# One projection moved behind the inverses' doublings in the order, and one expansion tied on VectorE

## The chip, the cores and the metric

One core of one Trainium2 chip runs the whole program. The metric is the device time of one execution in microseconds; lower is better. Engines are named as in the profile: PE (TensorE), DVE (VectorE), ACT (ScalarE), POOL (GpSimd) and SP (SyncE, here only a DMA queue).

## The reference

One layer of a hybrid decoder in float32, over 1024 prompt tokens and 64 sample tokens (8 sequences of 8):

```
h = x + 1/2 SwiGLU1(rmsnorm(x));  n = rmsnorm(h);  proj = n @ w_in
qkv, z, a, b, q_s, k_s, v_s = split(proj)
o_g = gated delta rule(silu(causal_conv(qkv)), a, b)   # 4 heads of 128, chunked, triangular solve
o_s = sliding-window attention(rope(q_s), rope(k_s), v_s)  # 8 query heads of 64, 2 kv heads, window 128
h += concat(rmsnorm(o_g) * silu(z), o_s) @ w_out
h += 1/2 SwiGLU2(rmsnorm(h));  h += sigmoid(rmsnorm(h) @ ple_gate) * (p @ ple_proj);  y = rmsnorm(h)
```

In the delta rule each chunk of 128 tokens needs the inverse of a lower triangular 128 x 128 matrix per head; then a state S is carried from chunk to chunk. The outputs are y, the states, the convolution's last rows and the attention's caches.

## The kernel before, in words

All 1088 tokens lie along the free axis, in four parts of 272 columns. A projection of w_in by one block of 128 output columns is a tile T, 0 to 21. It takes 4 parts of 24 products (8 blocks of the inner dimension, times three products of high and low halves): 96 matmuls of 128x128 on 128x272, in `proj` (L762), each part in one PSUM buffer of pool pps (two buffers, tag m). DVE then multiplies the part by the norm's factor into SBUF (`plain`, L781, or the convolution's `ev_pre`, L823). Tiles 0 to 11 feed the convolution, 12 to 15 are z, 16 to 19 the attention's queries (xq), 20 its keys (xk), 21 its values. A query or key tile then goes through `rope`: two multiplications and an addition of 128x1088 and four small DMAs.

The weights of a tile arrive by one DMA on SP's queue and are split into halves on ACT and POOL. Two split weights are held at a time; `next_weight` (L1455) after each tile asks for the one two places further on.

The inverses: `solve` (L961) inverts the 32x32 blocks on the diagonals for all chunks on DVE and writes them to DRAM (scrX). `levels` (L998), for a pair of chunks each ("lv", i, b: chunks 2i and 2i+1, in the SBUF tiles from b on), loads the blocks (`load_x`, L991), spreads them over a 128x128 block diagonal (`expand`, L985, on DVE: Em from the first set, Dm from the second) and doubles the block size twice, 32 to 64 to 128. One doubling of a chunk is a group of products plv<-lv,AT (a step's first), a mask on DVE, a second group of products, a subtraction on DVE, and after the first doubling a transpose (L1040) copied by ACT. Pairs 0, 2 and 3 use the same SBUF tiles (9 to 12), so pair 2 waits for pair 0; pair 1 has tiles 4 to 7 and runs beside pair 0. The PSUM pool of each chunk of each pair is a number in a table (`gps`, L932): plv00, plv01 and plv10 are 0, plv11 is 1, plv20 is 3 and plv21 is 4, which is pps, the pool of the projections.

`chain` (L1087, "go") is a step of the state, chunk by chunk: products pKS, pv and pS, with DVE and ACT between them, and pqS, the query with the state. `prep` ("pre") loads a chunk's operands, `outp` ("out") finishes its output.

The order of all this is written by hand in the list ORDER, walked at L1488. It is the order of the program, and it gives the priorities to a planner, which then orders each engine's queue by costs of its own; queues are fixed when the kernel runs. Dependencies without a semaphore (NOSYNC) bind only the order on one engine. `mm` (L175) uses them: while a projection is being written (fill), its matmuls are placed behind gates, the last product of each group in `chain`, 22 to a gate (OPT q). A projection that is written while there are no gates yet isn't bound; tile 16 was one, tile 18 is the first that is bound.

Of the kernel before, what the change touches and what calls it, by code (L numbers as in the profile page):

```python
# [13 lines left out]
ALU = mybir.AluOpType  # L14
# [25 lines left out]
G_F1, G_MIX, G_F2, G_PLE, G_FIN, G_GDN, G_CONV = 0, 8, 16, 24, 32, 40, 41  # L40
G_DT, G_ALOG, G_SINK, G_SKS = 89, 93, 97, 105
NVEC = 107
ORDER = [('T', 5), ('co', 5), ('T', 6), ('co', 6), ('T', 4), ('co', 4), ('T', 7), ('T', 8), ('co', 7), ('sc',), ('co', 8), ('s1', 0), ('s1', 1), ('s1', 8), ('T', 9), ('s1', 4), ('s1', 5), ('s1', 6), ('T', 1), ('co', 9), ('s1', 7), ('co', 1), ('T', 10), ('s1', 3), ('s1', 2), ('T', 11), ('co', 10), ('so', 8, (8,)), ('so', 0, (6, 12, 2, 11)), ('T', 21), ('T', 0), ('co', 11), ('co', 0), ('lv', 0, 9), ('T', 2), ('T', 3), ('co', 3), ('co', 2), ('T', 20), ('cvo',), ('qs',), ('T', 16), ('pre', 0, 0), ('lv', 2, 9), ('lv', 1, 4), ('go', 0), ('pre', 1, 4), ('out', 0), ('lv', 3, 9), ('pre', 2, 0), ('pre', 3, 9), ('go', 1), ('go', 2), ('out', 2), ('go', 3), ('out', 1), ('out', 3), ('pre', 4, 0), ('go', 4), ('pre', 5, 4), ('out', 4), ('lvs',), ('pre', 8, 9), ('go', 5), ('out', 5), ('pre', 7, 4), ('pre', 6, 0), ('go', 6), ('go', 7), ('T', 18), ('end',), ('T', 17), ('out', 6), ('swa', 1, 0, 14), ('T', 14), ('out', 7), ('sa', 0, 8), ('swa', 2, 0, 6), ('sb', 0, 1), ('swa', 2, 1, 2), ('T', 12), ('sa', 1, 7), ('swa', 1, 2, 8), ('sb', 1, 4), ('swa', 0, 2, 3), ('swa', 1, 1, 5), ('swa', 0, 0, 14), ('T', 19), ('sa', 2, 13), ('sb', 2, 6), ('swa', 0, 1, 15), ('sa', 3, 2), ('sb', 3, 7), ('swa', 3, 2, 3), ('so8',), ('swa', 3, 0, 8), ('swa', 3, 1, 0), ('T', 15), ('T', 13), ('swa', 2, 2, 4), ('ml', 0, 0), ('ml', 1, 0), ('ml', 3, 0), ('swl', 16, 10), ('ml', 3, 1), ('ml', 2, 0), ('ml', 7, 0), ('ml', 4, 0), ('swa', 0, 3, 6), ('ml', 6, 0), ('ml', 5, 0), ('sws', 1, 13), ('ml', 1, 1), ('ml', 2, 1), ('swa', 1, 3, 2), ('swa', 2, 3, 9), ('sws', 0, 5), ('swa', 3, 3, 12), ('ml', 4, 1), ('ml', 5, 1), ('wo', 0, 3), ('wo', 4, 0), ('ml', 0, 1), ('swe',), ('wo', 5, 2), ('wo', 6, 6), ('wo', 3, 4), ('ml', 6, 1), ('wo', 7, 1), ('wo', 1, 5), ('wo', 2, 7), ('ml', 7, 1)]
NOSYNC = mybir.DependencyInfo(mybir.DependencyClass.NoSync, mybir.DependencyReason.DATA)
CHAIN = ("so", "lv", "lvs", "pre", "go", "out", "qs")
OPT = dict(m=2, a=1, c=1, g=2, t=2, pkk0=1, pkk1=2, pdc0=0, pdc1=0, plv00=0, plv01=1, plv10=0, plv11=2, plv20=0, plv21=1, plv30=0,
           plv31=2, pkq=0, pW=0, pKS=1, W=0, hc=0, hs=0, hw=0, q=0, ne=6, wp=0, px=3, po=3, pxo=3, pxl=3, pol=3, pxol=3, pv=2, pS=2, pqS=0, pov=0, pxg=0, pb=0, pvs=0, pSs0=0, pSs4=2, pr0=1, pr1=1, pt0=1, pt1=4,
           zp=1)
# [101 lines left out]
def decoder_layer(ctx: ExitStack, tc: tile.TileContext, mix_off, a, o):  # L150
    nc = tc.nc
    V, S, T, G = nc.vector, nc.scalar, nc.tensor, nc.gpsimd
# [13 lines left out]
    ident = cst.tile([P, P], F32, name="ident")  # L166
# [1 line left out]
    ones = ones_r.bitcast(F32)  # L168
    vecs = cst.tile([P, NVEC], F32, name="vecs")

    gates, filled, fill = [], [0], [False]

    newest = [None]

    def mm(out, lhsT, rhs, start=True, stop=True, pin=False):  # L175
        i = T.matmul(out, lhsT=lhsT, rhs=rhs, start=start, stop=stop)  # L176
        if pin and newest[0] is not None:
            tc.add_manual_dep(i.ins, newest[0], NOSYNC, reason="keeps its place behind the products that come first")
        newest[0] = i.ins.name
        if fill[0] and OPT["q"]:  # L180
            at = filled[0] // OPT["q"]
            if at < len(gates):
                tc.add_manual_dep(i.ins, gates[at], NOSYNC, reason="fills the time up to the next step of the state")
                filled[0] += 1
        return i

    def bc(ap, axis, n):
        return ap.unsqueeze(axis).to_broadcast(list(ap.shape[:axis]) + [n] + list(ap.shape[axis:]))
# [561 lines left out]
    cvs, cvo = cvt_[:, :, :24], cvt_[:, :, 24:]  # L750
# [234 lines left out]
    def expand(c, xc, t):  # L985
        n, m = (P, C("bm")) if c < 8 else (NS, C("bm8")[:NS])
        nb = m.shape[1]
        V.tensor_tensor(out=t.rearrange("p h (b r) -> p h b r", b=nb), in0=bc(xc, 2, nb),
                        in1=bc(bc(m, 1, 4), 3, n // nb), op=ALU.mult)

    def load_x(t, c):  # L991
        n, src, q0, bl = (P, scrX, 4 * c, BL) if c < 8 else (NS, scrXs, 0, DT)
# [2 lines left out]
            nc.sync.dma_start(out=xc[:, w], in_=src[w].rearrange("(q p r) -> p q r", p=n, r=bl)[:, q0 : q0 + 4])  # L995
        return xc

    def levels(cs2, b0):  # L998

        R2 = range(len(cs2))  # L1000
        lv = [B(b0 + j, [2, 4, P], "lv") for j in R2]
        Em, Dm = [t[:, 0] for t in lv], [t[:, 1] for t in lv]
        Pt = B(b0 + 2, [2, 4, P], "Pm")
        At = B(b0 + 3, [2, 4, P], "AT")
        H = P // 2

        def halves(x, b, odd):

            lead = "p h" if len(x.shape) == 3 else "p"
            x = x.rearrange(f"{lead} (a two b) -> {lead} a two b", two=2, b=b)  # L1010
            return x[:, :, :, odd] if len(x.shape) == 5 else x[:, :, odd]

        def bank(name, b):
            t = gps("plv", H, key=f"plv{cs2[0] // 2}{name}")
            return t, t.rearrange("p h (a b) -> p h a b", b=b)

        for j, c in enumerate(cs2):
            xc = load_x(Pt[:, j], c)
            nc.sync.dma_start(out=At[:, j], in_=scr_a(c))
            expand(c, xc[:, 0], Em[j])  # L1020
            expand(c, xc[:, 1], Dm[j])
        Pc = [Pt[:, j, :, :H] for j in R2]
        for b in (32, 64):
            mask = halves(C(f"M{b}"), b, 0)
            for j in R2:
                pP, pv_ = bank(j, b)
                for hh in range(4):
                    mm(pP[:, hh], At[:, j, hh], halves(Dm[j][:, hh], b, 0))
                V.tensor_tensor(out=Pc[j].rearrange("p h (a b) -> p h a b", b=b), in0=pv_, in1=bc(mask, 1, 4), op=ALU.mult)
            if b != 64:  # L1030
                for j in R2:
                    pD, pv_ = bank(j, b)
                    for hh in range(4):
                        mm(pD[:, hh], Em[j][:, hh], Pc[j][:, hh])
                    dst = halves(Dm[j], b, 0)
                    V.tensor_tensor(out=dst, in0=dst, in1=pv_, op=ALU.subtract)
                for j in R2:
                    pE = gps("plv", key=f"plv{cs2[0] // 2}{j}")
                    for hh in range(4):
                        T.transpose(pE[:, hh], Dm[j][:, hh], ident)  # L1040
                    S.copy(halves(Em[j], b, 1), halves(pE, b, 1))
            else:
# [44 lines left out]
    def chain(I):  # L1087

        c, n = I["c"], I["n"]
# [4 lines left out]
        if S0 is not None and not OPT["W"]:  # L1094
            pk = gps("pKS")[:n]
            for hh in range(4):
                last = mm(pk[:, hh], I["k"][:, hh], S0[:, hh])
            gates.append(last.ins.name)
            for hh in range(4):
                V.scalar_tensor_tensor(out=I["v"][:, hh], in0=pk[:, hh], scalar=cs["egcn"][:n, c, hh : hh + 1], in1=I["v"][:, hh],  # L1100
                                       op0=ALU.mult, op1=ALU.add)
        pv = gps("pv")[:n]
        for hh in range(4):
            W = S0 is not None and OPT["W"]
            last = mm(pv[:, hh], I["XT"][:, hh], I["v"][:, hh], stop=not W)
            if W:
                last = mm(pv[:, hh], I["k"][:, hh], S0[:, hh], start=False)
        gates.append(last.ins.name)
        S.copy(I["vw"][:, :2], pv[:, :2])
        V.tensor_copy(I["vw"][:, 2:], pv[:, 2:])  # L1110
        pS = gps("pS")
        for hh in range(4):
            last = mm(pS[:, hh], I["kd"][:, hh], I["vw"][:, hh])
        gates.append(last.ins.name)
        if S0 is None:
            V.tensor_copy(S1, pS)
        else:
# [288 lines left out]
    def pre(i, c):  # L1406
        I[c] = prep(i, c)
# [28 lines left out]
    def conv_state():  # L1436
        nc.scalar.dma_start(out=o["conv"], in_=cvo)

    ops = dict(co=lambda m: conv_out(m, cvt[m]), sc=scalars, qs=q_scalars, s1=stage1, so=solve,
               lv=lambda i, b: levels((2 * i, 2 * i + 1), b), lvs=levels_sample, pre=lambda c, b: pre(b, c), go=go, out=out,  # L1440
               end=end_state, cvo=conv_state, swa=swa, swe=swa_end, swl=swa_load, sws=swa_sample, sa=sam_a, sb=sam_b,
               so8=sam_out, ml=mix_split)
    first_tile = next(x[1] for x in ORDER if x[0] == "T")
# [198 lines left out]
```

## Time and profile before

| | us |
|---|---|
| median of 3 runs | 2319.13 (2317.98 to 2320.62) |
| profiled execution | 2326.01 |
| its span, first to last instruction | 2324.2 |

| engine | busy us of the span |
|---|---|
| PE | 2256.2 |
| DVE | 1411.5 |
| ACT | 869.2 |
| POOL | 530.3 |

The profile is of one execution, and an engine's busy time is an average over stages with different limits. Matmuls overlap and their ends are modelled, so a busy PE may be one at half its clock; the granted clock is read beside it. Times of rows are us from the span's start.

### The profile page before, as it was taken

The numbers are of one execution on the slowest core, as the hardware profiler recorded it, in microseconds if no ns is written. First come the engines' busy times: TensorE is split into PE (matmuls) and PEld (weight loads), VectorE is DVE, ScalarE is ACT, GpSimd is POOL, SyncE is SP. The second block draws the span as 40 slices with busy tenths as digits, with TensorE's granted clock in tenths as the row PEclk, the third lists the DMA queues.
The fourth block names the chain that finished last, engine by engine and source line by source line (L and its number), as shares of the span: only waits on it lengthen the run. The fifth ranks groups of instructions, "written<-read, shape, count | busy, mean of one in ns | idle before, by whom it ended". The sixth has DMA issues, their size and how long they took to land. (4 is left out here: it accounts for less than half of the span.)

```text
span 2324.2 us, 43652 instructions
## 1 busy us (share of the span) xinstructions
PE 2256.2 (97%) x17472; PEld 2206.9 (95%) x17472; DVE 1411.5 (61%) x2719; ACT 869.2 (37%) x1694; POOL 530.3 (23%) x448
## 2 busy tenths in 40 slices
PE   8999999999999999989999999999999999999997
PEld 7999999999999899889987799999999999999997
DVE  8866655965423567955554537865556684443567
ACT  6433333434412364322234524433333344332444
POOL 0133332210000334332321000233333220011324
PEclk9999999999999999979987799999999999999998
DMA  5322222366433246265543365322222248433223
GB/s 189 106 80 84 76 74 75 125 230 221 156 104 102 86 140 173 90 165 161 158 146 95 93 195 186 112 76 76 76 84 73 76 157 275 136 111 107 95 95 129
DMA packets 180090, 289.85 MB, mean 125 GB/s; under 512 B 33359, under 2 KB 89679, under 8 KB 179887
## 3 DMA queue, kind: packets, MB, share of 16 engines
q1 hardware_dynamic: 126976, 224.77, 30.8%
q10 hardware_dynamic: 52911, 62.29, 7.7%
q8 instruction: 137, 2.24, 0.4%
q14 instruction: 66, 0.54, 0.1%
HBM read 219.48 MB, written 66.83 MB: 123 GB/s over the span
## 5 line engine op out<-in xcount | busy, mean ns | idle before, releaser
L176 PE MATMUL pd<-xa,t 128*128 128x272 f32 x4224 | 532.8, 289 | 5.5 <-DVE s L462 4.7
L176 PEld LDWEIGHTS pd<-xa,t 128*128 128x128 f32 x4224 | 531.9, 189 | 6.4 <-DVE s L462 5.2
L176 PE MATMUL pm<-xn,t 128*128 128x272 f32 x2112 | 300.2, 298 | 16.1 <-DVE pre L823 7.0
L206 DVE TENSOR_TENSOR t<-raw,t 128x1024 fp32r<-128x1024 f32 x126 | 160.2, 1272 | 247.4 <-ACT t L205 246.8
L176 PEld LDWEIGHTS pm<-xn,t 128*128 128x128 f32 x2112 | 280.5, 195 | 21.9 <-DVE pre L823 8.4
L205 ACT CAST t<-raw 128x1024 fp32r<-128x1024 f32 x148 | 155.0, 1047 | 313.1 <-PE pd L176 236.8
L176 PE MATMUL pS<-lT,hS 128*128 128x272 f32 x900 | 260.4, 289 | 0.0
L176 PE MATMUL pS<-hT,lS 128*128 128x272 f32 x900 | 260.1, 289 | 0.0
L176 PE MATMUL pS<-hT,hS 128*128 128x272 f32 x900 | 259.1, 288 | 0.0
L176 PE MATMUL pA<-hB,lA 128*128 128x272 f32 x600 | 172.6, 288 | 0.0
L206 DVE TENSOR_TENSOR lA<-raw,hA 128x512 fp32r<-128x512 f32 x171 | 137.0, 804 | 58.4 <-ACT hA L205 52.2
L176 PE MATMUL pA<-hB,hA 128*128 128x272 f32 x600 | 172.5, 288 | 0.0
L176 PE MATMUL pA<-lB,hA 128*128 128x272 f32 x600 | 172.1, 287 | 0.0
L176 PEld LDWEIGHTS pS<-hT,hS 128*128 128x128 f32 x900 | 169.6, 188 | 0.0
L176 PEld LDWEIGHTS pS<-hT,lS 128*128 128x128 f32 x900 | 169.3, 188 | 0.0
L176 PEld LDWEIGHTS pS<-lT,hS 128*128 128x128 f32 x900 | 169.2, 188 | 0.0
L205 ACT CAST hA<-raw 128x512 fp32r<-128x512 f32 x171 | 105.8, 620 | 160.2 <-PE pA L176 121.0
L205 ACT CAST hS<-raw 128x512 fp32r<-128x512 f32 x145 | 89.4, 620 | 176.5 <-PE pS L176 153.8
L258 POOL TENSOR_TENSOR r<-r,sq 128x544 f32<-128x544 f32 x28 | 47.1, 1682 | 426.7 <-ACT sq L257 425.5
L206 DVE TENSOR_TENSOR lS<-raw,hS 128x512 fp32r<-128x512 f32 x145 | 127.9, 882 | 18.0 <-ACT hS L205 5.2
L462 DVE TENSOR_TENSOR u<-u,pS 128x272 f32<-128x272 f32 x225 | 91.2, 432 | 54.4 <-PE pS L176 54.1
L176 PEld LDWEIGHTS pA<-lB,hA 128*128 128x128 f32 x600 | 113.0, 188 | 0.0
(364 smaller groups left out, 4712.1 us busy)
## 6 DMA issues: line engine op xcount, KB each, us to landing
raw<-in_gu SPq DMA_DIRECT2D x114, 512.0 KB
raw<-in_dn SPq DMA_DIRECT2D x88, 512.0 KB
scrU<-act ACTq DMA_DIRECT2D x88, 272.0 KB
a<-scrU SPq DMA_DIRECT2D x88, 272.0 KB
raw<-in_gate SPq DMA_DIRECT2D x24, 512.0 KB
raw<-in_w_in SPq DMA_DIRECT2D x22, 512.0 KB
raw<-in_w_out SPq DMA_DIRECT2D x14, 512.0 KB
h<-in_x SPq DMA_DIRECT2D x2, 2176.0 KB
```

What stands on the lines that cost most here:

```text
L176: i = T.matmul(out, lhsT=lhsT, rhs=rhs, start=start, stop=stop)
L205: S.copy(hi, src)
L206: return eng.tensor_tensor(out=lo, in0=src, in1=hi.bitcast(F32), op=ALU.subtract)
L258: G.tensor_tensor(out=self.acc[c], in0=self.acc[c], in1=sq, op=ALU.add)
L462: i_ = V.tensor_tensor(out=I[c][out], in0=I[c][x], in1=pt_, op=ALU.add)
```

## The change

In ORDER, ("lv", 0, 9) moves from behind tile 0's convolution to behind tile 20, that is past tiles 2, 3 and 20 and the transposes of 3 and 2. ("T", 16) moves from ahead of ("pre", 0, 0) to behind ("lv", 2, 9) and ("lv", 1, 4). Cut to these entries, the list changes so:

```
- ... ('co', 0), ('lv', 0, 9), ('T', 2), ('T', 3), ('co', 3), ('co', 2), ('T', 20), ('cvo',), ('qs',),
-     ('T', 16), ('pre', 0, 0), ('lv', 2, 9), ('lv', 1, 4), ('go', 0), ('pre', 1, 4), ...
+ ... ('co', 0), ('T', 2), ('T', 3), ('co', 3), ('co', 2), ('T', 20), ('lv', 0, 9), ('cvo',), ('qs',),
+     ('pre', 0, 0), ('lv', 2, 9), ('lv', 1, 4), ('T', 16), ('go', 0), ('pre', 1, 4), ...
```

The gates become a list of places, one per matmul. Pairs 1 and 2 of the inverses add 8 places after each of 6 groups (four first products, two transposes), 96 in all, which are tile 16's; the state's groups add 22 each as before, so tile 18 and those after it keep theirs. Both expansions of chunk 0 are ordered on DVE behind the last eviction of the last tile written by `plain`, which is tile 20's.

```
-        if fill[0] and OPT["q"]:
-            at = filled[0] // OPT["q"]
-            if at < len(gates):
-                tc.add_manual_dep(i.ins, gates[at], NOSYNC, reason="fills the time up to the next step of the state")
+        if fill[0]:
+            if filled[0] < len(places):
+                tc.add_manual_dep(i.ins, places[filled[0]], NOSYNC, reason="fills the time up to the next step of the state")
                 filled[0] += 1
         return i
+    def gate(i, n):
+        places.extend([i.ins.name] * n)
...
     def plain(dst):
         def ev(pm, c0, wd, r):
-            V.tensor_tensor(out=dst[:, c0 : c0 + wd], in0=pm, in1=r, op=ALU.mult)
+            i = V.tensor_tensor(out=dst[:, c0 : c0 + wd], in0=pm, in1=r, op=ALU.mult)
+            last_ev[0] = i.ins.name
...
     def expand(c, xc, t):
...
+        if c == 0:
+            tc.add_manual_dep(i.ins, last_ev[0], NOSYNC, reason="behind the evictions that are ready while the blocks are on their way")
...
-    def levels(cs2, b0):
+    def levels(cs2, b0, fillers):
...
                 for hh in range(4):
-                    mm(pP[:, hh], At[:, j, hh], halves(Dm[j][:, hh], b, 0))
+                    last = mm(pP[:, hh], At[:, j, hh], halves(Dm[j][:, hh], b, 0))
+                if fillers:
+                    gate(last, fillers)
...
                     for hh in range(4):
-                        T.transpose(pE[:, hh], Dm[j][:, hh], ident)
+                        last = T.transpose(pE[:, hh], Dm[j][:, hh], ident)
+                    if fillers:
+                        gate(last, fillers)
...
-            gates.append(last.ins.name)
+            gate(last, OPT["q"])
...
-               lv=lambda i, b: levels((2 * i, 2 * i + 1), b), ...
+               lv=lambda i, b: levels((2 * i, 2 * i + 1), b, 8 if i in (1, 2) else 0), ...
```

## Rows read from the trace of the kernel before

**Rows 1.** The page: busy time of each engine, share of the span, instructions.
```profile
PE 2256.2 (97%) x17472; PEld 2206.9 (95%) x17472; DVE 1411.5 (61%) x2719; ACT 869.2 (37%) x1694; POOL 530.3 (23%) x448
```

**Rows 2.** The page: granted clock of PE in 40 slices of 58.1 us, in tenths.
```profile
PEclk9999999999999999979987799999999999999998
```

**Rows 3.** Stretches: length; PE, PEld, DVE, ACT, POOL busy; granted clock; DMA share; GB/s.
```profile
997.30:1001.50 4.20, 4.20 (x35) 4.02 (x33) 0.00 (x0) 2.44 (x9) 2.38 (x1) 1.00 1.00 277
1001.50:1004.75 3.25, 0.04 (x1) 0.00 (x0) 1.70 (x4) 1.56 (x9) 0.00 (x0) 0.82 1.13 338
1004.75:1012.80 8.05, 8.05 (x44) 8.00 (x45) 4.16 (x8) 1.10 (x6) 1.00 (x1) 0.65 0.85 217
1012.80:1028.50 15.70, 15.70 (x144) 15.46 (x142) 8.62 (x20) 4.37 (x17) 7.83 (x4) 1.00 0.38 84
1028.50:1030.20 1.70, 0.09 (x2) 0.06 (x2) 1.70 (x3) 0.00 (x0) 1.70 (x1) 1.00 1.05 266
1030.20:1047.40 17.20, 17.20 (x88) 16.63 (x89) 7.54 (x15) 1.12 (x3) 4.11 (x4) 0.52 0.60 185
1047.40:1055.30 7.90, 7.90 (x75) 7.58 (x73) 4.10 (x10) 1.94 (x8) 2.04 (x2) 0.96 0.80 256
997.30:1055.30 58.00, 53.17 (x382) 51.75 (x380) 27.81 (x56) 12.53 (x51) 19.06 (x12) 0.79 0.67 189
```

**Rows 4.** DVE in order of time: start, duration, instruction, idle before it and releaser.
```profile
995.65 0.43 DVE L783 TENSOR_TENSOR xk<-pm,r 128x272 f32<-128x272 f32 x1
1003.05 1.29 DVE L988 TENSOR_TENSOR lv<-Pm,ctile 128x512 f32<-128x512 f32 x2 [6.97 <-DMA Pm<-scrX]
1004.26 0.43 DVE L783 TENSOR_TENSOR xk<-pm,r 128x272 f32<-128x272 f32 x1
...
1006.86 1.90 DVE L988 TENSOR_TENSOR lv<-Pm,ctile 128x512 f32<-128x512 f32 x3 [1.21 <-DMA Pm<-scrX]
...
1028.46 1.29 DVE L1196 TENSOR_TENSOR xq<-xq,rope 128x1088 f32<-128x1088 f32 x1 [1.33 <-DMA rot<-xq]
...
1051.28 0.42 DVE L1029 TENSOR_TENSOR Pm<-plv,ctile 128x256 f32<-128x256 f32 x1 [0.86 <-PE plv L176]
```

**Rows 5.** PE in order of time, from tile 20's end to level 2.
```profile
999.38 1.03 PE L855 MATMUL ptk<-ident,cv 128*128 128x128 f32 x8
...
1004.75 4.45 PE L176 MATMUL pm<-xn,t 128*128 128x272 f32 x18 [3.21 <-DVE xk L783]
...
1012.80 1.90 PE L176 MATMUL plv<-lv,AT 128*128 128x64 f32 x16
...
1025.46 1.14 PE L176 MATMUL plv<-lv,Pm 64*64 64x64 f32 x16
...
1037.50 1.97 PE L176 MATMUL plv<-lv,AT 128*128 128x64 f32 x8
```

**Rows 6.** SP's queue in order of time: the loads of the inverses' blocks.
```profile
997.39 2.62 SPq L995 DMA_DIRECT2D Pm<-scrX  x3
```

**Rows 7.** PE in order of time, in the state steps.
```profile
1054.47 1.06 PE L176 MATMUL pKS<-St,qk 128*128 128x128 f32 x8
...
1078.41 0.68 PE L176 MATMUL plv<-lv,Pm 64*64 64x64 f32 x8
...
1080.01 1.06 PE L176 MATMUL pqS<-St,qk 128*128 128x128 f32 x8
...
1132.60 4.77 PE L176 MATMUL pm<-xn,t 128*128 128x272 f32 x36
```

**Rows 8.** Stretches behind the state steps, columns as in rows 3.
```profile
1171.40:1229.00 57.60, 54.27 (x331) 46.74 (x330) 30.09 (x88) 22.31 (x65) 11.57 (x7) 0.85 0.40 132
1229.00:1266.20 37.20, 33.31 (x198) 26.46 (x198) 18.13 (x64) 21.03 (x59) 4.54 (x3) 0.91 0.38 116
1266.20:1301.00 34.80, 34.80 (x113) 24.75 (x112) 13.63 (x56) 11.44 (x44) 1.91 (x1) 0.50 0.25 79
```

**Rows 9.** The same stretch, projections' buffers alone: length, PE, PEld, DVE, clock, DMA.
```profile
1229.00:1266.20 37.20, 0.87 (x5) 0.68 (x5) 0.44 (x1) 0.91 0.38 116
```

More of the change, by code (lines that the diff above doesn't have):

```diff
@@ L42 @@
 NVEC = 107
-ORDER = [('T', 5), ('co', 5), ('T', 6), ('co', 6), ('T', 4), ('co', 4), ('T', 7), ('T', 8), ('co', 7), ('sc',), ('co', 8), ('s1', 0), ('s1', 1), ('s1', 8), ('T', 9), ('s1', 4), ('s1', 5), ('s1', 6), ('T', 1), ('co', 9), ('s1', 7), ('co', 1), ('T', 10), ('s1', 3), ('s1', 2), ('T', 11), ('co', 10), ('so', 8, (8,)), ('so', 0, (6, 12, 2, 11)), ('T', 21), ('T', 0), ('co', 11), ('co', 0), ('lv', 0, 9), ('T', 2), ('T', 3), ('co', 3), ('co', 2), ('T', 20), ('cvo',), ('qs',), ('T', 16), ('pre', 0, 0), ('lv', 2, 9), ('lv', 1, 4), ('go', 0), ('pre', 1, 4), ('out', 0), ('lv', 3, 9), ('pre', 2, 0), ('pre', 3, 9), ('go', 1), ('go', 2), ('out', 2), ('go', 3), ('out', 1), ('out', 3), ('pre', 4, 0), ('go', 4), ('pre', 5, 4), ('out', 4), ('lvs',), ('pre', 8, 9), ('go', 5), ('out', 5), ('pre', 7, 4), ('pre', 6, 0), ('go', 6), ('go', 7), ('T', 18), ('end',), ('T', 17), ('out', 6), ('swa', 1, 0, 14), ('T', 14), ('out', 7), ('sa', 0, 8), ('swa', 2, 0, 6), ('sb', 0, 1), ('swa', 2, 1, 2), ('T', 12), ('sa', 1, 7), ('swa', 1, 2, 8), ('sb', 1, 4), ('swa', 0, 2, 3), ('swa', 1, 1, 5), ('swa', 0, 0, 14), ('T', 19), ('sa', 2, 13), ('sb', 2, 6), ('swa', 0, 1, 15), ('sa', 3, 2), ('sb', 3, 7), ('swa', 3, 2, 3), ('so8',), ('swa', 3, 0, 8), ('swa', 3, 1, 0), ('T', 15), ('T', 13), ('swa', 2, 2, 4), ('ml', 0, 0), ('ml', 1, 0), ('ml', 3, 0), ('swl', 16, 10), ('ml', 3, 1), ('ml', 2, 0), ('ml', 7, 0), ('ml', 4, 0), ('swa', 0, 3, 6), ('ml', 6, 0), ('ml', 5, 0), ('sws', 1, 13), ('ml', 1, 1), ('ml', 2, 1), ('swa', 1, 3, 2), ('swa', 2, 3, 9), ('sws', 0, 5), ('swa', 3, 3, 12), ('ml', 4, 1), ('ml', 5, 1), ('wo', 0, 3), ('wo', 4, 0), ('ml', 0, 1), ('swe',), ('wo', 5, 2), ('wo', 6, 6), ('wo', 3, 4), ('ml', 6, 1), ('wo', 7, 1), ('wo', 1, 5), ('wo', 2, 7), ('ml', 7, 1)]
@@ new lines @@
+ORDER = [('T', 5), ('co', 5), ('T', 6), ('co', 6), ('T', 4), ('co', 4), ('T', 7), ('T', 8), ('co', 7), ('sc',), ('co', 8), ('s1', 0), ('s1', 1), ('s1', 8), ('T', 9), ('s1', 4), ('s1', 5), ('s1', 6), ('T', 1), ('co', 9), ('s1', 7), ('co', 1), ('T', 10), ('s1', 3), ('s1', 2), ('T', 11), ('co', 10), ('so', 8, (8,)), ('so', 0, (6, 12, 2, 11)), ('T', 21), ('T', 0), ('co', 11), ('co', 0), ('T', 2), ('T', 3), ('co', 3), ('co', 2), ('T', 20), ('lv', 0, 9), ('cvo',), ('qs',), ('pre', 0, 0), ('lv', 2, 9), ('lv', 1, 4), ('T', 16), ('go', 0), ('pre', 1, 4), ('out', 0), ('lv', 3, 9), ('pre', 2, 0), ('pre', 3, 9), ('go', 1), ('go', 2), ('out', 2), ('go', 3), ('out', 1), ('out', 3), ('pre', 4, 0), ('go', 4), ('pre', 5, 4), ('out', 4), ('lvs',), ('pre', 8, 9), ('go', 5), ('out', 5), ('pre', 7, 4), ('pre', 6, 0), ('go', 6), ('go', 7), ('T', 18), ('end',), ('T', 17), ('out', 6), ('swa', 1, 0, 14), ('T', 14), ('out', 7), ('sa', 0, 8), ('swa', 2, 0, 6), ('sb', 0, 1), ('swa', 2, 1, 2), ('T', 12), ('sa', 1, 7), ('swa', 1, 2, 8), ('sb', 1, 4), ('swa', 0, 2, 3), ('swa', 1, 1, 5), ('swa', 0, 0, 14), ('T', 19), ('sa', 2, 13), ('sb', 2, 6), ('swa', 0, 1, 15), ('sa', 3, 2), ('sb', 3, 7), ('swa', 3, 2, 3), ('so8',), ('swa', 3, 0, 8), ('swa', 3, 1, 0), ('T', 15), ('T', 13), ('swa', 2, 2, 4), ('ml', 0, 0), ('ml', 1, 0), ('ml', 3, 0), ('swl', 16, 10), ('ml', 3, 1), ('ml', 2, 0), ('ml', 7, 0), ('ml', 4, 0), ('swa', 0, 3, 6), ('ml', 6, 0), ('ml', 5, 0), ('sws', 1, 13), ('ml', 1, 1), ('ml', 2, 1), ('swa', 1, 3, 2), ('swa', 2, 3, 9), ('sws', 0, 5), ('swa', 3, 3, 12), ('ml', 4, 1), ('ml', 5, 1), ('wo', 0, 3), ('wo', 4, 0), ('ml', 0, 1), ('swe',), ('wo', 5, 2), ('wo', 6, 6), ('wo', 3, 4), ('ml', 6, 1), ('wo', 7, 1), ('wo', 1, 5), ('wo', 2, 7), ('ml', 7, 1)]
@@ L169, in decoder_layer @@
     vecs = cst.tile([P, NVEC], F32, name="vecs")
-    gates, filled, fill = [], [0], [False]
+    places, filled, fill = [], [0], [False]
+    last_ev = [None]
     newest = [None]
@@ L987, in expand @@
         nb = m.shape[1]
-        V.tensor_tensor(out=t.rearrange("p h (b r) -> p h b r", b=nb), in0=bc(xc, 2, nb),
-                        in1=bc(bc(m, 1, 4), 3, n // nb), op=ALU.mult)
+        i = V.tensor_tensor(out=t.rearrange("p h (b r) -> p h b r", b=nb), in0=bc(xc, 2, nb),
+                            in1=bc(bc(m, 1, 4), 3, n // nb), op=ALU.mult)
+        if c == 0:
+            tc.add_manual_dep(i.ins, last_ev[0], NOSYNC, reason="behind the evictions that are ready while the blocks are on their way")
     def load_x(t, c):
@@ L1107, in chain @@
                 last = mm(pv[:, hh], I["k"][:, hh], S0[:, hh], start=False)
-        gates.append(last.ins.name)
+        gate(last, OPT["q"])
         S.copy(I["vw"][:, :2], pv[:, :2])
@@ L1113, in chain @@
             last = mm(pS[:, hh], I["kd"][:, hh], I["vw"][:, hh])
-        gates.append(last.ins.name)
+        gate(last, OPT["q"])
         if S0 is None:
@@ L1439, in decoder_layer @@
     ops = dict(co=lambda m: conv_out(m, cvt[m]), sc=scalars, qs=q_scalars, s1=stage1, so=solve,
-               lv=lambda i, b: levels((2 * i, 2 * i + 1), b), lvs=levels_sample, pre=lambda c, b: pre(b, c), go=go, out=out,
+               lv=lambda i, b: levels((2 * i, 2 * i + 1), b, 8 if i in (1, 2) else 0), lvs=levels_sample, pre=lambda c, b: pre(b, c), go=go, out=out,
                end=end_state, cvo=conv_state, swa=swa, swe=swa_end, swl=swa_load, sws=swa_sample, sa=sam_a, sb=sam_b,
```

## The prediction

> **What bounds the kernel now.** I read the page first: PE is busy 97% of the span [rows 1], so time can only go where PE waits or runs slowly. The row of granted clocks says where: full nearly everywhere but in the 18th slice (988 to 1046 us), the 21st to 23rd (1162 to 1336) and the last [rows 2], the first two where the inverses, and later the attention, are mixed with projections. I then cut that stretch into windows [rows 3]. From 997.3 (end of tile 20's products) to 1055.3 (the second state step) PE does tile 16, the transposes of tiles 3 and 2, levels 0, 1 and 2 and the first state step. Busy time times clock, added over the seven windows, is 4.2 + 0.0 + 5.2 + 15.7 + 0.1 + 8.9 + 7.6 = 41.8 us of work at 2.4 GHz in 58.0 us: 16.2 us are lost, 4.8 by waiting and 11.4 by the 1.2 GHz level.
>
> The reader should see three losses. From 1001.5 to 1004.75 PE stands; its queue's head is tile 16's second part, which needs a PSUM buffer that tile 20's last eviction frees. That eviction (1004.26) stands on DVE behind two expansions that waited 6.97 us for the inverses' blocks [rows 4]. The low clock follows, until about 1011 (0.65 in the window to 1012.8). From 1028.5 to 1030.2 PE does nothing while DVE runs the rope of tile 16 (1.29 us) ahead of a subtraction [rows 4], and then comes 1030.2 to 1047.4: PE busy all the time at a clock of 0.52, on the small products of levels 1 and 2 and one state step [rows 3].
>
> **The change part by part.** *The tied expansion.* DVE runs tile 20's last eviction when its products end, so the wait of 3.2 us before tile 16's second part goes. But tile 16 is no longer there to profit. The expansions of pair 0 need their blocks: the second set of three is released at 1006.86 [rows 4], four loads behind the ones issued at 997.39 [rows 6]. In program order the loads of level 0 move behind the weight loads of tiles 2, 3 and 20; I cost this at nothing, since what they wait for is the solve and not the queue (if a weight load slips between, some 1.2 us, what DVE waited for the last of these loads). The first expansion waits for the same blocks as before; what is behind it on DVE are the other expansions, which wait for them too.
>
> *The hole.* So PE has, from 997.3 until the first product of level 0, only 18 transposes: 8 took 1.03 us [rows 5], 2.3 us in all. The first product is ready when chunk 0's second expansion ends, 1006.86 + 0.7 (one of the three's 1.90, with its end) plus some 0.2, about 1007.8, instead of 1012.80 [rows 5]: the levels start 5.0 us earlier, but 10.5 us hold 2.3 us of work: **8.2 us lost**. Of tile 16 nothing runs here; before, most of it did, and the rest among level 0's products.
>
> *Tile 16 among the doublings.* 96 products at 4.77/36 [rows 7] are 12.7 us. The first 48 are ordered behind level 2's six marked groups, the rest behind level 1's. The text of the kernel speaks against their running there. All parts of a projection use the two buffers of one PSUM pool, and so does the second chunk of level 2 (plv21 is 4, that pool), five times, all five ahead of tile 16 in program order. Whether buffers go round in program order the trace can show: the product of the query with the state of step 1 needs the state that its neighbour pKS used at 1054.47, and runs at 1080.01, just after level 3's last products at 1078.41 [rows 7], whose second chunk shares its pool and stands ahead of it in the program. Buffers do seem to be handed out in program order. Then tile 16's first part waits until level 2's last but one bank is evicted, which was at 1051.28 [rows 4]: it comes behind the doublings, not among them.
>
> *The levels without filler.* The remaining work is 41.8 - 12.7 - 2.3 = 26.8 us, of which 3.6 (1051.7 to 1055.3) can follow tile 16's start: 23.2 us of small products stand between 1007.8 and it. PE comes to them out of the hole; after the waits that end at 1004.75 and 1030.2 the rows show the 1.2 GHz level each time [rows 3], so I start there. How long? Bounds from rows: 8.05 us at 0.65 (2.8 lost; the products after that wait were tile 16's), 17.2 us at 0.52 (8.3 lost; the same products as here), 34.8 us at 0.50 (17.4 lost; the attention's small products with no projection among them [rows 8, 9]). I take the middle of the last two, 26 us: **13 us lost**, because the products are those of the 17.2 but, unlike then, no projection precedes them.
>
> When the clock is back (about 1034) 10 us of work are left, mostly level 2. It reuses level 0's tiles, and from level 0's last product (1025.46 + 1.14) to level 2's first (1037.50) the loads and expansions took 10.9 us [rows 5]. Level 0 should end near 1026 at the low level, so level 2 starts near 1037, level 1 covers all but 1 to 2 us, and the two chunks of level 2 alone wait for each other's evictions: **4 us** of waits (estimate; 1.5 if only the load gap counts, 8 if the clock returns early and the chain alone sets the pace).
>
> Tile 16's own evictions (four), rope, next weight split and five DMAs on ACT's queue, and on SP's queue the load of the weight two ahead, move from 1005 to 1034 into the state steps. No tile waits for them soon. Their cover is DVE's idle time (it is idle half of 997.3 to 1055.3 [rows 3]); uncovered, one rope ahead of a chain step costs the 1.7 us of that window. I take nothing.
>
> *Sum of the stretch.* 8.2 + 13 + 4 = 25.2 us lost against 16.2: **9 us later** at equal work.
>
> *What comes back.* The state steps order the later projections by 22 as before, so about a projection more is left at 1171 and runs among the attention's products. There PE is not short of loss: 37.2 - 33.31 x 0.91 = 6.9 us in 1229 to 1266.2 and 17.4 to 1301 [rows 8], almost without projections [rows 9]. Lower bound 0; upper about 12, half of the 24.3. I take 2: the tail that moves in reaches only from 1229 to about 1240, and the average clock there is 0.91.
>
> Net **+7 us**. The profiled execution took 2326.01 us (span 2324.2 and 1.8 around it), which would be 2333; it stands 0.3% above the median of the runs, 2319.13, so the forecast is **2326**.
>
> **The rivals.** *The clock returns at once.* This is level 0 to 2 at 2.4 GHz after 8 us (2.8 lost); then the chain sets the pace, and the waits are nearer 7. 8.2 + 2.8 + 7 - 16.2 - 2 is about 0: 2319. For it: from 1047.4 the clock is 0.96 on such products [rows 3]. Against it: 17.2 us without a wait at 0.52. The Trainium skill, "TensorE: Matmul & The Clock Gate", section "Why this matters for your kernels", says that matmuls issued back to back keep the PE warm and that waiting between bursts makes it cold. By that rule the hole is a fault of this change and dense doublings are a cure; the trace agrees on the hole, and on the cure only after 1047. By the rule alone the time is this rival's.
>
> *It does what it says.* If buffers are not handed out in order, 48 products of tile 16 fill level 2's waits (4 us back) and end the slow stretch some 6 us sooner (3 us): +7 - 7 = 0: 2319. Against it: the row at 1080.01.
>
> *Low clock until tile 16.* Then 23.2 us of small products run at 1.2 GHz throughout: 23.2 lost, no waits beside it, 2.8 more until tile 16 has raised the clock: 8.2 + 23.2 + 2.8 - 16.2 - 2 = +16: 2335. For it: the 34.8 us at 0.50.
>
> *The late stage takes it in (the other side).* If the projection that is left over keeps the clock up between 1229 and 1301, where 24.3 us are lost, more than 9 us come back and the sign turns; from 14 on it is measurable. At 18 it is +9 - 18 = -9: 2310. For it: 34.8 us at 0.50 with no projection [rows 8, 9]. Against it: nothing ties the leftover to that place; it runs as soon as it can, just behind 1229.
>
> **How the numbers follow.** A change under 0.2% (4.6 us) is about what a measurement of this kernel can't tell from none. Forecast 0.36, its own range 2322 to 2330, about one in eight of it under the bound; clock at once 0.14; as it says 0.14; low until tile 16 0.14; late stage 0.22. Slower: 0.31 + 0.14 = 0.45, and 0.02 from the two at zero, 0.47. Same: 0.05 + 0.23 = 0.28. Faster: 0.22 and 0.03, 0.25. The range runs from the late stage to the low clock, 2309 to 2335.
>
> **What would show it.** In the changed profile: tile 20's last eviction right after its products; PE nearly idle with transposes from about 997 to 1008; level 0's first product near 1008; a granted clock near 0.5 from there for 20 to 35 us; tile 16's products in one run after level 2's last but one eviction, not in eights between the level's groups; about a projection more of products after the last state step. Wrong I am if tile 16's eights stand among level 2's products, if the clock is full by 1016, or if the stretch from 1229 to 1301 has lost its 0.50.

## The result, and the profile after

| | before | after |
|---|---|---|
| median, 16 runs each | 2315.72 us (2300.43 to 2328.88) | 2329.64 us (2321.66 to 2342.99) |
| ratio | | 1.007, 95% interval 1.005 to 1.0091 |
| span of the profiled execution | 2324.2 us | 2327.3 us |

The change makes the kernel 0.7% slower, 14 us by the medians and 16 by the ratio. The forecast was 2326 us, 7 above before.

The page of the kernel after: PE's row of busy times, and the granted clock in 40 slices, now of 58.2 us.

```profile
PE 2262.1 (97%) x17472; PEld 2215.5 (95%) x17472; DVE 1408.9 (61%) x2719; ACT 870.1 (37%) x1694; POOL 532.3 (23%) x448
...
PEclk9999999999999999968999899999999999999999
```

PE has as many instructions as before and 5.9 us more of busy time [rows 1]. The clock is low in the 18th slice (989.1 to 1047.3 us), lower than before, and in the 19th, where it was full; of the 21st to 23rd, which read 8, 7 and 7, only the 23rd is still below, at 8 [rows 2]. Stretches of the kernel after, with the columns of [rows 3]; tile 20's products end at 1002.40 here, and 1079.46 is the state's second step, the point of equal work. The last two lines are stretches of [rows 8].

```profile
1002.40:1012.65 10.25, 3.23 (x18) 2.40 (x17) 3.59 (x7) 5.50 (x26) 3.35 (x2) 0.67 1.04 280
1012.65:1028.20 15.55, 14.28 (x66) 13.90 (x66) 7.32 (x15) 2.83 (x14) 5.52 (x3) 0.50 0.46 119
1028.20:1064.56 36.36, 36.36 (x187) 34.76 (x186) 12.29 (x28) 1.86 (x5) 1.04 (x1) 0.50 0.46 129
1064.56:1078.80 14.24, 14.24 (x106) 14.24 (x105) 7.32 (x21) 1.61 (x8) 2.04 (x2) 0.90 0.25 60
...
1002.40:1079.46 77.06, 68.77 (x380) 65.96 (x378) 30.96 (x71) 12.44 (x53) 11.94 (x8) 0.60 0.49 133
...
1229.00:1266.20 37.20, 37.20 (x262) 32.32 (x261) 17.25 (x62) 20.17 (x55) 3.27 (x2) 1.00 0.31 95
1266.20:1301.00 34.80, 34.80 (x153) 25.49 (x151) 16.89 (x60) 18.63 (x56) 5.53 (x3) 0.66 0.45 146
```

The same products take 77.1 us instead of 58.0 [rows 3]. Busy time times clock is 2.2 + 7.1 + 18.2 + 12.8 + 0.7 = 41.0 us, so 36.1 are lost: 8.1 in the hole, 7.1 + 18.2 = 25.3 by the 1.2 GHz level while the doublings run without a projection, 1.3 by waits among them, 1.4 until tile 16 has brought the clock back. PE in order of time in the same stretch:

```profile
994.68 7.81 PE L177 MATMUL pm<-xn,t 128*128 128x272 f32 x48 [2.07 <-DVE xk L787]
1002.33 1.03 PE L860 MATMUL ptk<-ident,cv 128*128 128x128 f32 x8
...
1012.65 1.97 PE L177 MATMUL plv<-lv,AT 128*128 128x64 f32 x8 [3.98 <-DVE lv L993]
...
1063.52 1.11 PE L177 MATMUL plv<-lv,Pm 64*64 64x64 f32 x8
1064.56 7.53 PE L177 MATMUL pm<-xn,t 128*128 128x272 f32 x48
1071.94 0.83 PE L177 MATMUL pov<-Y,X 128*128 128x128 f32 x6
1072.52 6.26 PE L177 MATMUL pm<-xn,t 128*128 128x272 f32 x48
...
1079.46 1.11 PE L177 MATMUL pKS<-St,qk 128*128 128x128 f32 x8
```

Tile 16 runs behind level 2's last group as one run of 96 products, but for six others between its halves; not one of its eights stands among the doublings. A group of 8 products of level 0 takes 1.97 us, where 16 took 1.90 before [rows 5]. DVE at the end of tile 20:

```profile
1000.49 0.43 DVE L787 TENSOR_TENSOR xk<-pm,r 128x272 f32<-128x272 f32 x1
1007.49 0.69 DVE L993 TENSOR_TENSOR lv<-Pm,ctile 128x512 f32<-128x512 f32 x1 [6.58 <-DMA Pm<-scrX]
1008.11 0.43 DVE L787 TENSOR_TENSOR xk<-pm,r 128x272 f32<-128x272 f32 x1
1008.46 1.28 DVE L993 TENSOR_TENSOR lv<-Pm,ctile 128x512 f32<-128x512 f32 x2
```

Tile 20's last eviction (1008.11) still stands behind an expansion that waits 6.58 us. Only chunk 0's two expansions are tied; another chunk's, which is not, now comes first (with all expansions tied, below, the eviction runs at 1000.65, ahead of every expansion).

From equal work on, the 19.1 us shrink. The last product of the last state step comes 181.7 us after tile 20's end instead of 173.9: 11.3 us were made up among the state steps. 8.9 of these are put off, since 260 projection products are left then instead of 193 (67 at 4.77/36 [rows 7]). So 16.7 us remain, close to the 14 to 16 that the runs measure.

### The profile page after: what moved, and what is told of

The parts are those of the page before. It is cut to its first block, busy times and chain, and to the rows that moved or that the text cites. A ratio compares the mean times of both kernels' runs of the same rounds, so it can differ in the third digit from the quotient of the medians.

```text
span 2327.3 us, 43647 instructions
## 1 busy us (share of the span) xinstructions
PE 2262.1 (97%) x17472; PEld 2215.5 (95%) x17472; DVE 1408.9 (61%) x2719; ACT 870.1 (37%) x1694; POOL 532.3 (23%) x448
```

## The experiments

All ratios are against the kernel before, run beside them. Each run lists its span and its mean granted clock; "all runs" is the mean, over a kernel's runs, of the clock lost, span x (1 - clock), and of the rest of the span. The last two columns tell where the one profiled execution lost its clock: "levels" is 1000 to 1080 us, "attention" 1180 to 1380, each in windows of 20 us, (1 - granted clock) x 20 added up; "idle" is the time in which PE was not busy there.

| run | ratio (95% interval) | all runs: clock lost, rest | span of the profile | levels: clock, idle | attention: clock, idle |
|---|---|---|---|---|---|
| before | | 50.2, 2264.2 | 2324.2 | 12.0, 4.8 | 30.8, 8.1 |
| before again | | | 2328.8 | 12.0, 5.3 | 36.0, 8.8 |
| after | 1.007 (1.005 to 1.0091) | 70.3, 2261.2 | 2327.3 | 30.6, 8.3 | 17.2, 4.3 |
| tile 16 back | 1.0007 (0.9982 to 1.0031) | 45.2, 2264.1 | 2296.9 | 13.6, 6.5 | 1.8, 4.3 |
| only tile 16 moved | 1.0096 (1.0061 to 1.013) | 67.6, 2262.6 | 2320.5 | 29.0, 6.7 | 15.6, 5.5 |
| tile 16 not tied | 1.0095 (1.0061 to 1.0129) | 66.8, 2262.0 | 2322.1 | 30.8, 6.3 | 15.6, 6.9 |
| level 2 in another pool | 1.0165 (1.0132 to 1.0198) | 77.4, 2268.8 | 2352.0 | 24.0, 11.6 | 44.6, 7.2 |
| tile 16 among levels 0, 1 | 1.0105 (1.0072 to 1.0138) | 68.6, 2269.9 | 2340.6 | 12.2, 11.2 | 44.4, 5.3 |
| hole filled | 1.0054 (1.0025 to 1.0082) | 64.1, 2264.2 | 2315.6 | 20.6, 5.8 | 15.6, 1.7 |
| rope late | 1.0068 (1.0039 to 1.0097) | 66.7, 2265.8 | 2332.3 | 10.2, 5.9 | 36.8, 12.1 |
| tile 18 among levels 2, 1 | 1.0025 (0.9994 to 1.0055) | 53.9, 2265.2 | 2314.0 | 8.4, 7.2 | 20.4, 5.7 |
| all tied | 0.9978 (0.9947 to 1.001) | 46.7, 2263.5 | 2311.8 | | |
| chunk 3 late | 0.9971 (0.994 to 1.0001) | 51.3, 2260.2 | 2304.3 | 15.2, 3.9 | 15.6, 3.4 |
| chunk 3 late, again | 0.997 (0.9939 to 1.0002) | 46.6, 2261.2 | 2315.6 | 15.2, 4.9 | 17.0, 4.5 |

The profiled executions of tile 16 back, only tile 16 moved and tile 16 not tied are the fastest of their kernels' runs, and that of hole filled is the second fastest of twelve: they lose 9 to 11 us less clock than these runs do on average. The levels' column repeats between profiles (12.0 twice for before, 15.2 twice for chunk 3 late); the attention's has to be read with the third column beside it.

### Which part of the change costs: tile 16

**Tile 16 back**, level 0 late and the expansions of chunk 0 tied as in the change.

```
-    ('cvo',), ('qs',), ('pre', 0, 0), ... ('lv', 1, 4), ('T', 16), ('go', 0)
+    ('cvo',), ('qs',), ('T', 16), ('pre', 0, 0), ... ('lv', 1, 4), ('go', 0)
-               lv=lambda i, b: levels(..., b, 8 if i in (1, 2) else 0)
+               lv=lambda i, b: levels(..., b, 0)
```

> Tile 16 goes back to its old place, untied, and the levels give no places; level 0's later place in the list and the tie of chunk 0's expansions stay. Theory A (the loss comes from tile 16 having left the wait for the blocks and level 0): about the kernel before, 4 us less to 2 us more, and no stretch of more than 20 us at half clock between tile 20 and the first state step. Theory B (level 0's later place or the tie costs it): as the changed kernel, about 14 us over the kernel before.

It measured 1.0007: as before. **Only tile 16 moved** is the other half, against the changed kernel:

```
-    ('co', 0), ('T', 2), ... ('T', 20), ('lv', 0, 9), ('cvo',)
+    ('co', 0), ('lv', 0, 9), ('T', 2), ... ('T', 20), ('cvo',)
...
-        if c == 0:
-            tc.add_manual_dep(i.ins, last_ev[0], NOSYNC, ...)
```

> Level 0 goes back to its old place in the list and nothing is tied on DVE; only tile 16 is moved, with its places. Theory A: as the changed kernel, 10 to 18 us over the kernel before, with tile 16 in one run behind level 2. Theory B: within 4 us of the kernel before.

It measured 1.0096 and loses 29.0 us of clock in the levels, as the changed kernel does. So tile 16's new place is the whole loss, and the place of level 0 and the tie are worth nothing that shows here. **Tile 16 not tied** leaves the eights out:

```
-            fill[0] = True
+            fill[0] = bound          # False for tile 16
-               lv=lambda i, b: levels(..., b, 8 if i in (1, 2) else 0)
+               lv=lambda i, b: levels(..., b, 0)
```

> The changed kernel without the eights: tile 16 in its new place in the list but bound to nothing, and the levels give no places. Theory A: the eights bind nothing that the buffers don't bind already, so this is the changed kernel within 4 us, 10 to 18 us over the kernel before. Theory C (the eights hold tile 16 back): tile 16 runs before level 2 ends and most of the 14 us come back.

1.0095, with 30.8 us against 30.6: the eights bind nothing.

### Why the eights don't run, and what they would do

**Level 2 in another pool** changes one number of the table of PSUM pools.

```
-    plv21=4
+    plv21=3
```

> The changed kernel with level 2's second chunk in another PSUM pool (plv21 3 for 4), so that tile 16's buffers no longer come after it. Theory A with the buffers as the cause of the late run: tile 16 stands in eights among level 2's groups, and 5 to 9 us of the 14 come back. If the buffers are not what holds tile 16: one run behind level 2 as in the changed kernel, and 14 us over the kernel before.

PE of this kernel among level 2's groups (its tile 20 ends at 997.1):

```profile
1035.72 2.16 PE L177 MATMUL pm<-xn,t 128*128 128x272 f32 x8
...
1043.08 2.16 PE L177 MATMUL pm<-xn,t 128*128 128x272 f32 x8
...
1046.63 1.59 PE L177 MATMUL plv<-Pm,lv 128*128 128x64 f32 x8
...
1053.04 1.27 PE L177 MATMUL pm<-xn,t 128*128 128x272 f32 x8
...
1064.65 1.05 PE L177 MATMUL pS<-Y 128*128 128x128 f32 x8
```

The eights are there, so it was the order in which a pool's buffers are given out that held them, as forecast. Eight products take 2.16 us at 1043 and 1.27 at 1053: the clock returns near 1047, some 11 us after the first eight. But I had expected a gain, and the kernel is 1% slower than the changed one. In the two profiles the levels lose 6.6 us less of clock and 3.3 more by waiting; the attention loses 27.4 us more of clock and 2.9 more by waiting. Over all runs it is less lopsided: 7.1 us more of clock lost than in the changed kernel, and 7.6 us more of the rest.

**Tile 16 among levels 0 and 1** keeps the pools and puts the tile ahead of level 2 in the program.

```
-    ('lv', 2, 9), ('lv', 1, 4), ('T', 16), ('go', 0)
+    ('lv', 1, 4), ('T', 16), ('lv', 2, 9), ('go', 0)
-               ... 8 if i in (1, 2) else 0)
+               ... 8 if i in (0, 1) else 0)
```

> The change with tile 16 ahead of level 2 in the program and its eights tied among levels 0 and 1. The hole behind tile 20 stays. If the loss is that small products run at the 1.2 GHz level until projection products stand among them, the eights bring the clock back near 1025 instead of 1067 and some 8 to 10 of the 14 us are given back: ratio to before 1.001 to 1.004. If the hole alone makes the loss, the ratio stays at 1.007. If eights among the levels push the state steps back, as the run with another PSUM pool for level 2 suggests, it is 1.010 or more.

PE behind the hole:

```profile
1010.35 1.97 PE L177 MATMUL plv<-lv,AT 128*128 128x64 f32 x8 [4.15 <-DVE lv L993]
1012.07 2.16 PE L177 MATMUL pm<-xn,t 128*128 128x272 f32 x8
...
1021.03 1.00 PE L177 MATMUL plv<-Pm,lv 128*128 128x64 f32 x8
...
1061.35 0.71 PE L177 MATMUL plv<-lv,Pm 64*64 64x64 f32 x8 [1.36 <-DVE Pm L1038]
```

In its own stretch the mechanism works: the clock is back at 1021, 11 us after the hole, the levels lose 12.2 us of clock as before the change, and level 2 and tile 16 are through 62.2 us after tile 20's end (999.86 to 1062.06) instead of 76.4 in the changed kernel. Then the attention takes it all, 44.4 us against 17.2; over all runs, too, this kernel loses as much clock as the changed one (68.6 and 70.3). The rest of its span is 8.7 us longer, of which the profile shows 2.9 as waits in the levels. The measured 1.0105 is the last rival's number, but not by its cause: the last state step ends 178.1 us after tile 20's end, only 4.2 later than before, with 189 projection products left (193 before).

### Is it the pause or the small products?

**Hole filled** adds 72 products that nothing reads.

```
+    def dummy(w):                                   # called behind tile 20
+        pm = proj_ps(0, 4)
+        for ci in range(3):
+            acc3(pm[:, : CH[ci][1]], [blocks(w)[k] + nm.x(ci, k) for k in range(KD)])
```

> The change with 72 more products of 128x272, tile 20's again, written behind tile 20 into a PSUM buffer that nothing reads: 9.5 us of added work in the hole. If the pause is what drops the clock and small products keep the level that they come with, levels 0 to 2 run at the full clock: 23 us of loss become some 7 us of waits, level 0 starts up to 2 us later, and the kernel is about 14 us faster than the changed one in spite of the added work: ratio to before about 1.001. If small products lose the clock by themselves, whatever stands ahead of them, it is low again by 1020 and the ratio is 1.007 to 1.009.

```profile
1007.28 1.63 PE L177 MATMUL pm<-xn,t 128*128 128x272 f32 x11
1008.88 2.00 PE L177 MATMUL plv<-lv,AT 128*128 128x64 f32 x16
1013.24 0.71 PE L177 MATMUL pkq<-qk 128*128 128x128 f32 x4 [2.35 <-DMA qk<-scrT]
...
1017.99 3.68 PE L177 MATMUL plv<-Pm,lv 128*128 128x64 f32 x16 [3.49 <-DVE Pm L1038]
...
1055.80 0.60 PE L1049 MATMUL plv<-ident,lv 128*128 128x128 f32 x4
```

Level 0 begins at the full clock (16 products in 2.00 us) and comes out of two pauses of 2.35 and 3.49 us at half of it (16 in 3.68). So small products did not lose the clock at once, and it fell across two pauses; the hole is one of several pauses, and filling it only puts the fall off to 1018. The full level is back near 1055, after 38 us at half clock without a projection. The trace doesn't part the theories, since "low again by 1020" was the second one's sign. The measured 1.0054, up to 1.0082, leaves out the 1.001 of the first and not the 1.007 of the second, and the profiled execution, at 2317.38, stands 15 us under the median of its twelve runs.

### The attention stage

**Before again** is the kernel before, unchanged.

> The kernel before, unchanged, for a second profile. If the low clock from 1200 to 1320 of its first profile (about 30 us lost) is of that execution and not of the program, this one differs there by more than 5 us, and its span differs by as much; if it is the program's, it shows the same windows again.

Nearly the same windows and a span 4.6 us longer, short of the bound of 5 us: no answer. Both profiled executions of before lie high among its 86 runs beside the experiments (2298.64 to 2340.48, median 2315.73), and the runs tell more. Each lists its mean granted clock, from 0.967 in the longest to 0.987 in the shortest; span x (1 - clock) has a correlation of 0.96 with the time. Averaged, the kernel before loses 50.2 us so, and its span less that is 2264.2; the changed kernel loses 70.3 and has 2261.2 left. The difference between the kernels is clock, 20.1 us, of which the levels hold 18.6.

The same stretch (1240 to 1300) in three kernels, a fence each, in the columns of [rows 3]: after, before again, and tile 16 back.

```profile
1240.00:1300.00 60.00, 60.00 (x329) 47.53 (x330) 27.02 (x98) 28.91 (x91) 6.88 (x4) 0.80 0.36 113
```

```profile
1240.00:1300.00 60.00, 55.76 (x264) 42.25 (x262) 28.07 (x114) 26.04 (x94) 4.53 (x3) 0.72 0.30 91
```

```profile
1240.00:1300.00 60.00, 59.34 (x408) 45.78 (x407) 38.74 (x155) 41.72 (x139) 7.20 (x5) 1.00 0.45 136
```

With tile 16 back the stage runs at full clock for all of it, though its last projection product is at 1235; its longest pause in this stretch is 0.32 us. (This is the execution that lost 34.5 us of clock, where the kernel's runs lose 45.2.) Before again has pauses of 3.54 and 4.10 us in the attention stage:

```profile
1197.81 1.64 PE L176 MATMUL pr<-ksT,sc 64*128 64x128 f32 x4 [3.54 <-DMA sc<-scrQ]
...
1247.67 0.82 PE L176 MATMUL pf<-oh,t 128*128 128x272 f32 x2 [4.10 <-ACT oh L205]
```

But these pauses are not what the long low stretch of this profile follows:

```profile
1253.00:1272.00 19.00, 18.86 (x119) 14.68 (x119) 10.17 (x42) 10.55 (x38) 0.50 (x1) 1.00 0.24 78
1274.00:1300.00 26.00, 26.00 (x96) 19.42 (x95) 12.01 (x50) 9.75 (x39) 0.00 (x0) 0.50 0.23 62
```

The clock is full for 19 us in which PE is busy for all but 0.14, and then low with PE busy all the time. So it is in ten of the fourteen profiles: the longest low stretch of the attention begins after 12 us or more at full clock in which PE did not pause for as much as 0.4 us. Small products can lose the clock without a pause.

**Rope late** takes two pauses out of the levels. In the run with all expansions tied (below), the rope of tile 16 stands on DVE ahead of two masks; PE waits 1.71 and 1.56 us for them, and the clock is low after the second. DVE, then PE, of that run:

```profile
1031.12 1.29 DVE L1209 TENSOR_TENSOR xq<-xq,rope 128x1088 f32<-128x1088 f32 x1 [1.97 <-DMA rot<-xq]
1032.33 0.42 DVE L1040 TENSOR_TENSOR Pm<-plv,ctile 128x256 f32<-128x256 f32 x1
```

```profile
1032.80 0.68 PE L177 MATMUL plv<-lv,Pm 64*64 64x64 f32 x8 [1.71 <-DVE Pm L1040]
...
1036.47 1.97 PE L177 MATMUL plv<-Pm,lv 128*128 128x64 f32 x8 [1.56 <-DVE Pm L1040]
```

```
-        rope(xq, xq)                      # tile 16, directly behind its products
+        late_q.append(xq)
...
+    ('lv', 2, 9), ('lv', 1, 4), ('rq',), ('go', 0)     # rq: rope, its DVE part behind level 2's last mask
```

> As the run with all expansions tied, and the rope of tile 16 (two DVE operations of 1.29 us, POOL's part and its DMAs) emitted behind level 1, its DVE part ordered behind level 2's last mask. If pauses of PE are what drops the clock and small products only keep the level that they find, the two pauses of 1.71 and 1.56 us behind the rope go, and with them most of the low level from 1036 to 1058 that followed: 3 us and some 10 us, ratio to before 0.992 to 0.995. If the small products lose the clock by themselves once tile 16's last products are through, only the pauses go: 0.997.

PE of this run, and its attention stage:

```profile
1031.78 1.06 PE L177 MATMUL plv<-lv,AT 128*128 128x64 f32 x8
1034.27 0.66 PE L1053 MATMUL plv<-ident,lv 128*128 128x128 f32 x4 [1.43 <-DVE lv L1049]
...
1039.91 1.81 PE L177 MATMUL plv<-lv,AT 128*128 128x64 f32 x8
```

```profile
1240.00:1300.00 60.00, 56.57 (x240) 43.23 (x238) 25.16 (x94) 22.02 (x78) 4.58 (x3) 0.64 0.27 84
```

The two pauses are gone, one of 1.43 us comes in their place, and the clock falls behind that one instead, near 1036 as it did with all expansions tied (0.66 from 1034.27 to 1040). So the run can't tell whether the pauses bring the fall. The levels still do well (10.2 us). The expectation on the time is missed by far, by the attention again: 36.8 us of clock and 12.1 idle, in a kernel that differs from the one with all expansions tied by one rope's place, and beyond that by what the planner made of it. All 12 of its runs took 2325 us or more, so this is the program's and not one execution's. What in the order decides it I haven't settled.

### A kernel that is faster

**All tied**: tile 16 in its old place, and every first expansion of chunks 0 to 3 behind tile 20's last eviction.

```
-        if c == 0:
-            tc.add_manual_dep(i.ins, last_ev[0], NOSYNC, ...)
+        if c == 0:
+            first_ev[0] = last_ev[0]
+        if c < 4:
+            tc.add_manual_dep(i.ins, first_ev[0], NOSYNC, ...)
```

> Tile 16 stands in its old place, without fillers; the places of level 0 stay as in the change, and all eight first expansions of chunks 0 to 3 (not only chunk 0's two) are ordered on DVE behind tile 20's last eviction. If the wait of 3.2 us of [rows 5] and the low clock behind it (2.8 us, the window to 1012.8 of [rows 3]) are a loss of their own, which the expansion of another chunk kept alive in the changed kernel, the eviction comes right after tile 20's products, tile 16 runs through, and the kernel is 4 to 6 us faster than before: ratio about 0.998. Rival: the products that start earlier only reach the wait for the inverses' blocks earlier, and the ratio is 1.000.

0.9978 was the number expected; the interval reaches past 1. **Tile 18 among levels 2 and 1** is this run with tile 18 as the filler and plv21=3:

```
-    ('lv', 1, 4), ('go', 0), ... ('go', 7), ('T', 18), ('end',)
+    ('lv', 1, 4), ('T', 18), ('go', 0), ... ('go', 7), ('end',)
```

> As the run with all expansions tied, and tile 18 moved from the state's end to behind level 1 in the order, its matmuls tied by eights among levels 2 and 1, with level 2's second chunk in PSUM pool 3 so that they can run there. Tile 16 fills the time behind tile 20, tile 18 the levels. If projection products keep the clock through 1030 to 1047, the 8.3 us lost there come back beside the 4 to 6 of the tie: ratio about 0.994. If the eights delay the first state steps by what they fill, and a projection is missed later among the state steps, it is 1.000 to 1.010.

It has the best clock of all in the levels (8.4 us) and is no faster: the second theory's number, and in part its cause. The last state step ends some 5 us later behind tile 20 than before's, though with 147 projection products left for 193. **Chunk 3 late** is the run with the rope late, and chunk 3's expansions behind pair 0's first masks.

```
+        if c == 3:
+            tc.add_manual_dep(i.ins, first_mask[1], NOSYNC, ...)
```

> As the run with the rope late, and chunk 3's expansions ordered on DVE behind pair 0's first two masks, so that the expansion that waited 3.01 us for its block no longer stands ahead of them. The pause of 1.45 us near 1016 goes; if the wait moves to pair 1's doublings, where tile 16's last parts cover it, the ratio is 0.001 below that of the run with the rope late; if pair 1 then starts too late for pair 0, equal to it or above.

> The kernel with all expansions tied, the rope late and chunk 3's expansions late, unchanged, timed again beside before. If its 0.9971 was its own and not the spread of single executions, the ratio is again 0.995 to 0.999, and the two intervals together leave 1.000 out; if not, it is 0.999 to 1.004.

PE of the first of the two:

```profile
999.62 1.04 PE L860 MATMUL ptk<-ident,cv 128*128 128x128 f32 x8
1000.41 3.63 PE L177 MATMUL pm<-xn,t 128*128 128x272 f32 x27
...
1008.35 1.94 PE L177 MATMUL plv<-lv,AT 128*128 128x64 f32 x16
...
1012.29 1.90 PE L177 MATMUL plv<-Pm,lv 128*128 128x64 f32 x16
```

The 3.21 us of [rows 5] and the pause near 1016 are gone. In their place PE waits 0.83 us at 1005.74 and 1.91 us at 1020.40, and behind the second the clock is at half until about 1052: the levels lose more clock than before (15.2 us for 12.0). 0.9971 and 0.997, in 12 runs each; taken together, with halves of 0.0031, that is 0.9971 with 0.0022 to either side: 0.3% faster than before and 1% faster than the change. Over the 24 runs the span without lost clock is 2260.7 against 2264.2, so the gain is mostly in the rest of the span, and hardly in the clock (48.9 us lost against 50.2). That it is the wait of [rows 5] isn't shown: by the last state step neither profile is ahead of before (171.5 and 177.2 us after tile 20's end with 211 projection products left, where before has 173.9 and 193), the idle time of the levels is about the same (3.9 and 4.9 us for 4.8 and 5.3), and what is smaller is the attention's (3.4 and 4.5 for 8.1 and 8.8). The step from 1.0068 to 0.9971 is not the 0.001 that I had expected of it; it is the attention again (15.6 and 17.0 us against 36.8).

## Why the prediction was right, and where it was not

The sign, the mechanism and the range held; the size was half, +7 us for 14 to 16. That the 2326 came within 4 us of 2329.64 is in part luck: it was counted from 2319.13, a median of three runs, and the 16 runs beside the change have 2315.72. By its own steps:

- *The hole.* 8.2 us were forecast, 8.1 measured, and the first product of level 0 came where forecast, 10.25 us after tile 20's end. Of the wait on DVE the step was wrong: the last eviction did not move up to the products' end, because one tie does not reach the other chunks' expansions. It cost nothing, since tile 16 had left.
- *Buffers in program order, tile 16 behind the doublings.* Right: one run of 96, and eights among level 2 only with another pool.
- *The levels without filler.* This is the step that was mis-sized. I took 26 us as the middle of two rows for the length of the low clock, 13 us lost; it was low all the way from 1012.65 to tile 16, 25.3 us lost. The rival "low clock until tile 16" had 23.2 and 2.8 (25.3 and 1.4 measured) and the sum nearest to the measured change, +16. Why the middle was no good value: the row of 17.2 us [rows 3] is itself a stretch that happened to recover. Without a projection the same products needed 17 us in before, 38 in the run with the hole filled, and over 50 here.
- *Waits in place of the low clock.* 4 us forecast, 1.3 measured: at half the clock PE is late, and DVE is not.
- *What comes back.* 2 us forecast. Of the 19.1 us at equal work 2.4 were made up by the last state step, besides the 8.9 put off: from 1080 to 1180 PE is busy 97.1 us at 1.00, where the same windows of before have 94.9 at 0.97. In the attention the two profiles suggest a return of 13.6 us of clock, but that is how the profiled execution of before fell out: over all runs the clock lost is 20.1 us more, and the levels alone account for 18.6.
- *What would show it.* The last test, that the stretch from 1229 to 1301 must keep its 0.50, went against the prediction: after reads 1.00 to 1266.2 and 0.66 from there, for 0.91 and 0.50. It was no good test, since that level differs from profile to profile: with tile 16 back, at a ratio of 1.0007, it is at 1.00. The low clock of the levels lasted longer than the 20 to 35 us named.

The rival by the Trainium skill, "TensorE: Matmul & The Clock Gate", section "Why this matters for your kernels" (back to back keeps warm, waiting between bursts makes cold), is half borne out: each fall shown here from 997 to 1040 stands behind a pause, but in the 36.36 us row above PE never waits and stays at 0.50, and in the attention the clock falls without a pause.

## What to carry to other kernels

A projection among small products can be worth more than its own time where it stands, since it brought the granted clock back wherever these runs have one there; before moving one, price the place that it leaves at half clock for as long as nothing of its kind stands there. Putting one there is no gain by itself: the three runs that did so among the doublings came out at 1.0105, 1.0165 and 1.0025. A tie on one engine's queue helps only as far as it holds everything that may go ahead, and a tie to places in a queue does nothing when PSUM buffers are given out in program order. Where the time of single executions follows their mean clock, compare medians of many runs, and don't read a gain or loss of one stage from two profiles unless the runs bear it out.

## What was not expected of the hardware

- Small products with PE busy all the time can run at 1.2 GHz for over 36 us (0.50, after) or at the full clock for the 60 us from 1240 to 1300 (1.00, tile 16 back). Which of the two isn't settled by pauses alone: from 997 to 1040 each fall shown stands behind one, but in the attention the clock falls without any in ten of fourteen profiles, as in the kernel after between 1268 and 1282, with no pause recorded from 1185 to 1309.
- One program varies by 1.8% from execution to execution (2298.64 to 2340.48 us in 86 runs of before), and nearly all of it is granted clock.
- In one execution, that of the run with all expansions tied, the row of the clock reads 0.95 in most windows and 0.931 in the mean, and its products take no longer: 33 of a projection in 4.35 us, where the run with chunk 3 late has 38 in 5.01, 0.132 us each in both. Its span is 2311.8 us. The table leaves this execution's clock out, of the levels, the attention and the mean over its runs, and the mean of the changed kernel's runs leaves out one that reads 0.927 at 2324.18 us.
